# First value weights of attention split during the last projection unit, first attention scores held behind the value products

## The chip, the core and the metric

The kernel runs on one core of a Trainium2 chip. Its five engines each take instructions in order from a queue of their own: TensorE (PE, matrix products), VectorE (DVE), ScalarE (ACT), GpSimd (POOL) and SyncE (SP, which here only issues DMAs). They wait for one another through semaphores. The metric is device time in microseconds (us) of one execution, and lower is better.

## The reference, cut to what matters

The program is one decoder block on 1024 tokens of 1024 channels in float32. What bears on the change is how the projections feed attention:

```python
h = rmsnorm(x, norm_mix[i])
proj = h @ w_in[i]
qa, ka, va, qb, fb, ib, gb, gate_a, gate_b = jnp.split(proj, IN_SPLITS, axis=-1)
ya = dilated_attention(qa, ka, va)       # 8 heads of 64: softmax over masked scores q k^T, times v
yb = hgrn2(qb, fb, ib, gb, lb_all[i], hg_norm[i])
merged = jax.nn.sigmoid(gate_a) * (ya @ w_a_up[i]) + jax.nn.sigmoid(gate_b) * (yb @ w_b_up[i])
x = x + merged @ w_out[i]
# then a SwiGLU block, a per-layer embedding and a last norm
```

`va` has 512 columns. The kernel makes it in two halves of 256 columns.

## The kernel before, in words

**Split products.** Every float32 operand of a product is split into a high part in the fp32r format and a low part, the rest. A product is then three matmuls: high by high, high by low, low by high. For a weight block `weight` (lines 165 to 173) issues a DMA from HBM into a raw tile `wr`, POOL rounds it to the high part `wh` (L171), and DVE subtracts to get the low part `wl` (L172).

**Memory slots.** Big tiles lie in 49 slots of 4 KB per partition, s0 to s48. A `Ring` hands out a fixed list of slots in turn. A tile that gets a slot waits for everything that still reads or writes the slot's tile before it.

**Projection units.** Twenty column tiles of `w_in` go through ten Winograd units of two tiles each (`winograd`, `proj_unit`). A unit makes seven products of 12 matmuls each in the order 1, 5, 7, 2, 3, 4, 6 (`ORDER`), so product 7 is its third. The weight side of a product is a tile `q`, split on ACT (L299) and DVE (L300) into slots 3 to 7. The token side of products 5, 7, 4 and 6 lies in tiles `B`, split once at the start and read by all ten units. Those of product 7 are in slots 41 to 44, and the tenth unit is the last to read them. Products 3 and 7 write the two halves of one PSUM tile `u`. Between product 7 and the products that add to that tile, DVE reads it (L335, into `v`).

**After a unit** DVE and POOL add the products up (L771 to L781) into tiles `pj` in slots 40, 47 and 8, and SP stores them to HBM (L794). The last unit stores `hgq_dram`; its first `pj` lies in slot 8.

**Start of attention** (from L840). `qk_parts` loads queries and keys of a head back from HBM (`qr`, `kl`) and splits them on ACT (L471, L472) and DVE (L474, L475). `v_gemm(0, ...)` (L489) loads and splits two weight tiles of the first half of `va` (the high parts in the ring of slots 3, 4, 5, the low parts in that of 8, 6, 7) and makes eight tiles of 128 tokens. Each has 24 matmuls of 256 columns (L484 to L486), goes to one of three PSUM banks b0 to b2, and is moved out by ACT (L499) and DVE (L500). `attend_rows` makes scores of 128 queries (L525, L526) in the one PSUM tile `sp`; DVE adds the mask and takes the row minimum (L538), ACT takes exp (L542), DVE the reciprocal of the sum (L543), and POOL scales (L544). `attend_values` transposes such rows on PE (L565) and multiplies them with the values (L557, L558). `fill` puts matmuls of other products (here gates, L192 to L194) between these steps.

**What sets the order.** The Tile framework orders each engine's queue ahead of time, from dependencies and its own estimates of durations, not in the order in which the code is written. `tc.issue_after(ins)` asks that instructions of a block stand behind `ins` in the queue of the engine of `ins`.

Of the kernel before, what the change touches and what calls it, by code (L numbers as in the profile page):

```python
# [20 lines left out]
P = 128  # L21
# [23 lines left out]
SCALE_A, SCALE_B = 0.9, (1.6, 1.3, 1.3, 1.3, 1.0)  # L45
# [8 lines left out]
class Ring:  # L54
# [7 lines left out]
    def next(self, shape, dtype, name):  # L62
        tag = self.tags[self.n % len(self.tags)]
        self.n += 1
        Ring.count += 1
        return self.pool.tile(list(shape), dtype, tag=tag, name=f"{name}_{Ring.count}")
# [49 lines left out]
def drain(gen):  # L116
    for _ in gen:
        pass
# [11 lines left out]
def block_kernel(ctx: ExitStack, tc: tile.TileContext, a: dict, out: bass.AP):  # L130
    nc = tc.nc
    pe, dve, act, pool = nc.tensor, nc.vector, nc.scalar, nc.gpsimd
# [7 lines left out]
    def ring(ids):  # L140
        return Ring(sb, [f"s{i}" for i in ids])
# [9 lines left out]
    ones = cp.tile([P, P], F32, name="ones")  # L151
# [8 lines left out]
    def f32(t):  # L160
        return t.bitcast(F32)
# [4 lines left out]
    def weight(src, shape, hi_ring=None, lo_ring=None):  # L166
        raw = RAW.next(shape, F32, "wr")
        nc.sync.dma_start(raw, src)
        hi = (hi_ring or HI).next(shape, F32R, "wh")
        lo = (lo_ring or LO).next(shape, F32R, "wl")  # L170
        pool.tensor_scalar(hi, raw, 1.0, 0.0, ALU.mult, ALU.add)  # L171
        dve.tensor_sub(lo, raw, f32(hi))  # L172
        return hi, lo

    def weight_parts(src, shape):

        raw, hi, lo = RAW.next(shape, F32, "wr"), HI.next(shape, F32R, "wh"), LO.next(shape, F32R, "wl")

        def part(j):
            ks = slice(4 * j, 4 * j + 4)  # L180
            nc.sync.dma_start(raw[:, ks], src[:, ks])
            pool.tensor_scalar(hi[:, ks], raw[:, ks], 1.0, 0.0, ALU.mult, ALU.add)
            dve.tensor_sub(lo[:, ks], raw[:, ks], f32(hi)[:, ks])

        return (hi, lo), part
# [174 lines left out]

    warm = MS.next([P, 512], F32, "warm")
    for _ in range(WARM):
        pe.matmul(warm[:, :P], ones, ones, start=True, stop=True)
    w_start = [weight_parts(a["w_in"][20 + t], [P, KD, P]) for t in range(NTOGETHER)]
    both = ps.tile([P, 2, 512], F32, tag="sp", name="start")
    banks = [ps.tile([P, 512], F32, tag=t, name=f"start_{t}") for t in ("b0", "b1", "b2", "ov")]
# [6 lines left out]
    def start_rights(j, i):  # L373

        for k in {5: (i,), 7: (i + 4,)}.get(j, ()):
            act.activation(xr8[k], xr8[k], AF.Identity, scale=vec[:, V_MIX + k : V_MIX + k + 1])
        right[j][i] = RIGHT[j](xr8, i, 4, ring([TB[j][i]]))

    def latest(engine):

        return next(i for i in reversed(nc.cur_bb.bb.instructions) if i.engine == engine)
# [47 lines left out]
    with tc.issue_after(last_split), tc.issue_after(last_square.ins):  # L429
        for i in range(4):  # L430
            start_rights(5, i)
# [46 lines left out]
    def nat_gemm(b, wts, t):  # L478

        ts_ = slice(t * P, (t + 1) * P)  # L480
        for k in range(KD):
            hi, lo = wts[k // 4]
            xh, xl = xg[k]
            pe.matmul(b, xh[:, ts_], hi[:, k % 4, :], start=(k == 0), stop=False)  # L484
            pe.matmul(b, xh[:, ts_], lo[:, k % 4, :], start=False, stop=False)  # L485
            pe.matmul(b, xl[:, ts_], hi[:, k % 4, :], start=False, stop=(k == KD - 1))  # L486
            yield 3 * 0.107

    def v_gemm(half, vs):  # L489
        wts = [weight(a["w_v"][half, j], [P, 4, 256]) for j in range(2)]  # L490
        for t in range(NTOK):
            if t % 2 == 0:
                vs.append(VR.next([P, 2, 4, 2, 64], F32R, "v"))
            v = vs[-1]
            b = MM.next([P, 512], F32, "mm")[:, :256]
            yield from nat_gemm(b, wts, t)
            bv = b.rearrange("p (h d) -> p h d", h=4)
            r = rn[:, t : t + 1]
            act.activation(v[:, t % 2, :, 0, :], bv, AF.Identity, scale=r)  # L499
            dve.scalar_tensor_tensor(  # L500
                v[:, t % 2, :, 1, :], bv, r, f32(v)[:, t % 2, :, 0, :], op0=ALU.mult, op1=ALU.subtract
            )
# [12 lines left out]
    def attend_rows(g, qkh, rows):  # L515

        q, kh, kl = qkh
        pr2 = None
        for i in range(4 * g, 4 * g + 4):
            n = (i + 1) * P  # L520
            sp = ps.tile([P, S], F32, tag="sp", name=f"sp{Ring.count}")
            k0 = 0
            for w in SEG[i + 1]:
                ks = slice(k0, k0 + w)
                pe.matmul(sp[:, ks], q[:, i * P : i * P + P], kh[:, ks], start=True, stop=False)  # L525
                pe.matmul(sp[:, ks], q[:, i * P : i * P + P], kl[:, ks], start=False, stop=True)  # L526
                k0 += w
            if g:
                pr = PR[1].next([P, S], F32, "p")
            elif i % 2 == 0:  # L530
                pr2 = PR[0].next([P, 2, 512], F32, "p")
                pr = pr2[:, 0]
            else:
                pr = pr2[:, 1]
            m = sm.tile([P, 1], F32, tag="m", name="m")
            den = sm.tile([P, 1], F32, tag="den", name="den")
            rd = sm.tile([P, 1], F32, tag="rd", name="rd")
            dve.tensor_tensor_reduce(  # L538
                out=pr[:, :n], in0=sp[:, :n], in1=NB[:, S - n :], op0=ALU.add, op1=ALU.min,
                scale=1.0, scalar=3e38, accum_out=m,  # L540
            )
            act.activation(pr[:, :n], pr[:, :n], AF.Exp, bias=m, scale=-1.0, accum_out=den)  # L542
            dve.reciprocal(rd, den)  # L543
            pool.tensor_scalar(pr[:, :n], pr[:, :n], rd, 0.0, ALU.mult, ALU.add)  # L544
            rows.append(pr)
            yield Y_ROW[0] + Y_ROW[1] * (i + 1) / 8
# [202 lines left out]
    units = [(j, j + 1) for j in range(0, 20, 2)]  # L749
# [12 lines left out]
    def proj_dst(j):  # L762
        if j < 8:
            return qk_dram[j]
        return hg_dram["fg"[j % 2]][j // 2 - 4] if j < 16 else hg_dram["q"][j - 16]

    rn = cp.tile([P, NTOK], F32, name="rn")
    for tiles in units:
        done = dict(proj_unit(right, TG))
        e0, e1 = (EO.next([P, S], F32, "pj") for _ in range(2))  # L770
        dve.tensor_add(e0[:, c1], done[3], done[6])  # L771
        dve.tensor_add(e1[:, c0], done[4], done[6])
        pool.tensor_add(e1[:, c1], done[7], done[6])
        if tiles[0] < 8:

            dve.scalar_tensor_tensor(e0[:, c0], done[2], -0.125, rs[:, c0], op0=ALU.mult, op1=ALU.mult)
            dve.scalar_tensor_tensor(e0[:, c1], e0[:, c1], -0.125, rs[:, c1], op0=ALU.mult, op1=ALU.mult)
        else:
            dve.tensor_mul(e0[:, c0], done[2], rs[:, c0])
            dve.tensor_mul(e0[:, c1], e0[:, c1], rs[:, c1])  # L780
        pool.tensor_mul(e1, e1, rs)  # L781
        if 8 <= tiles[0] < 16:
            hd = tiles[0] // 2 - 4
            k = EO.next([P, S], F32, "k")
            act.activation(e0, e0, AF.Sigmoid)
            pool.tensor_scalar(e0, e0, oml[:, hd : hd + 1], lb[:, hd : hd + 1], ALU.mult, ALU.add)
            pool.tensor_scalar(k, e0, -1.0, 1.0, ALU.mult, ALU.add)
            nc.sync.dma_start(hg_dram["k"][hd], k)
            for cs in halves:
                sg = EV.next([P, 512], F32, "sg")  # L790
                act.activation(sg, e1[:, cs], AF.Sigmoid)
                dve.tensor_mul(e1[:, cs], e1[:, cs], sg)
        for j, e in zip(tiles, (e0, e1)):
            nc.sync.dma_start(proj_dst(j), e)  # L794
        if tiles[0] == 6:

            diag = EO.next([P, NTOK, P], F32, "diag")
            rs3 = rs.rearrange("p (n t) -> p n t", n=NTOK)
            dve.tensor_mul(diag, rs3, ident.unsqueeze(1).to_broadcast([P, NTOK, P]))
            dve.tensor_reduce(out=rn, in_=diag, axis=mybir.AxisListType.X, op=ALU.add)  # L800
# [31 lines left out]
    fill = Filler()  # L832
# [7 lines left out]
    qk, vs, vn = {}, ([], []), ([], [])  # L840
# [2 lines left out]
    MM = pring("b0", "b1", "b2")  # L843
    NB = ring([47]).next([P, S], F32, "nb")
    nc.sync.dma_start(NB, a["nb"])
    drain(v_gemm(0, vs[0]))
    RAW, HI, LO = ring([0, 1]), ring([3, 4]), ring([8, 6])
    rows = []
    add_gates(2)
    v_last = fill.add(v_gemm(1, vs[1]))  # L850
    fill.along(attend_rows(0, qk[0, 0], rows), SCALE_A)
    groups = [(p, h, g) for p in range(NPAIR) for h in range(2) for g in range(2)]
    for (p, h, g), after in zip(groups, groups[1:] + [None]):
        if (p, h, g) == (2, 0, 0):
# [17 lines left out]
        rows = next_rows  # L872
# [477 lines left out]
```

## Time and profile before

| what | us |
|---|---|
| three runs | 1670.85, 1673.15, 1665.83 |
| their median | 1670.85 |
| the profiled execution | 1667.34 |
| its span, from the first to the last instruction | 1665.5 |
| PE busy in the span | 1604.8 (96%) |
| DVE busy | 1117.4 (67%) |
| ACT busy | 649.5 (39%) |
| POOL busy | 559.9 (34%) |

The profiled execution lies 3.5 us under the median of the runs and within their spread. The page of the profile gives each engine's busy time; the timeline gives each instruction's start and length; the table by stage gives busy time and the clock that TensorE was granted (1.00 is 2.4 GHz, 0.50 is 1.2 GHz) in a stretch. A start is in us from the beginning of the span.

### The profile page before, as it was taken

The numbers are of one execution on the slowest core, as the hardware profiler recorded it, in microseconds if no ns is written. First come the engines' busy times: TensorE is split into PE (matmuls) and PEld (weight loads), VectorE is DVE, ScalarE is ACT, GpSimd is POOL, SyncE is SP. The second block draws the span as 40 slices with busy tenths as digits, with TensorE's granted clock in tenths as the row PEclk, the third lists the DMA queues.
The fourth block names the chain that finished last, engine by engine and source line by source line (L and its number), as shares of the span: only waits on it lengthen the run. The fifth ranks groups of instructions, "written<-read, shape, count | busy, mean of one in ns | idle before, by whom it ended". The sixth has DMA issues, their size and how long they took to land.

```text
span 1665.5 us, 21614 instructions
## 1 busy us (share of the span) xinstructions
PE 1604.8 (96%) x7968; PEld 1332.7 (80%) x7968; DVE 1117.4 (67%) x1673; ACT 649.5 (39%) x1128; POOL 559.9 (34%) x413
## 2 busy tenths in 40 slices
PE   9899998999999999999999999999999999998996
PEld 7687787898998888888887888888888778775786
DVE  8955664678665566765557666666777668798536
ACT  6523332467552011532345333333333554444334
POOL 2555652223322111114354343444554000034214
PEclk9999998999999999999999999999999999999998
DMA  5232343332124322533432323334444887654202
GB/s 197 76 115 102 139 157 116 96 90 72 52 92 146 109 102 77 196 133 114 153 113 83 113 90 99 111 114 140 152 140 163 276 292 232 233 154 128 63 1 101
DMA packets 84778, 213.54 MB, mean 128 GB/s; under 512 B 9408, under 2 KB 16320, under 8 KB 84672
## 3 DMA queue, kind: packets, MB, share of 16 engines
q1 hardware_dynamic: 84528, 212.14, 39.0%
q8 instruction: 62, 1.02, 0.3%
q14 instruction: 44, 0.36, 0.1%
q10 hardware_dynamic: 144, 0.02, 0.0%
HBM read 155.51 MB, written 56.62 MB: 127 GB/s over the span
## 4 chain that ended last, share of the span: by engine, by line
PE 47%; DVE 7%; DMA 4%; issue 2%; ACT 2%; POOL 1%; DVEq 0%; SPq 0%; POOLq 0%; ACTq 0%
PE u L275 8%; PE u L276 8%; PE u L277 8%; PE mm L194 5%; PE mm L192 5%; PE mm L193 5%; DVE B L236 2%; PE g L666 1%; DMA w<-w_dn 1%; DVE q L1028 1%; PE dnb L277 1%; PE dnb L275 1%; PE dnb L276 1%; DMA st<-t_dram 1%; DMA st<-first_dram 1%
## 5 line engine op out<-in xcount | busy, mean ns | idle before, releaser
L275 PE MATMUL u<-B,q 128*128 128x512 f32 x776 | 303.8, 394 | 5.6 <-ACT m L333 3.6
L276 PE MATMUL u<-B,q 128*128 128x512 f32 x776 | 304.4, 392 | 3.7 <-DVE B L236 3.7
L277 PE MATMUL u<-B,q 128*128 128x512 f32 x776 | 303.4, 391 | 1.9 <-DVE q L300 1.9
L275 PEld LDWEIGHTS u<-B,q 128*128 128x128 f32 x776 | 146.6, 189 | 41.5 <-ACT m L333 8.2
L276 PEld LDWEIGHTS u<-B,q 128*128 128x128 f32 x776 | 146.7, 189 | 35.4 <-DVE B L236 5.2
L277 PEld LDWEIGHTS u<-B,q 128*128 128x128 f32 x776 | 146.6, 189 | 32.9 <-DVE q L300 2.3
L299 ACT CAST q<-s 128x512 fp32r<-128x512 f32 x128 | 79.5, 622 | 157.6 <-PE u L277 145.6
L300 DVE TENSOR_TENSOR q<-s,q 128x512 fp32r<-128x512 f32 x128 | 107.5, 842 | 49.2 <-ACT q L299 48.1
L192 PE MATMUL mm<-xh,wh 128*128 128x512 f32 (+1 forms) x352 | 138.1, 392 | 0.1
L194 PE MATMUL mm<-xh,wl 128*128 128x512 f32 (+1 forms) x352 | 132.0, 375 | 1.8 <-DVE wl L172 1.7
L193 PE MATMUL mm<-xl,wh 128*128 128x512 f32 (+1 forms) x352 | 131.4, 373 | 0.0
L171 POOL TENSOR_SCALAR wh<-wr 128x1024 fp32r<-128x1024 f32 (+1 forms) x55 | 57.3, 1044 | 203.9 <-PE mm L193 100.1
L300 DVE TENSOR_TENSOR q<-w,q 128x512 fp32r<-128x512 f32 x96 | 85.0, 886 | 60.2 <-ACT q L299 60.0
L193 PE MATMUL mm<-l,wh 128*128 128x512 f32 (+1 forms) x296 | 115.0, 389 | 1.3 <-DVE l L910 0.9
L192 PE MATMUL mm<-h,wh 128*128 128x512 f32 (+1 forms) x296 | 114.7, 389 | 0.9 <-POOL wh L171 0.8
L194 PE MATMUL mm<-h,wl 128*128 128x512 f32 (+1 forms) x296 | 114.0, 386 | 1.0 <-DVE wl L172 1.0
L299 ACT CAST q<-w 128x512 fp32r<-128x512 f32 x96 | 59.7, 622 | 121.8 <-PE u L277 69.1
L544 POOL TENSOR_SCALAR p<-p,rd 128x128 f32<-128x128 f32 (+3 forms) x64 | 53.1, 831 | 144.3 <-DVE rd L543 126.4
L1082 POOL TENSOR_TENSOR us<-v 128x512 f32<-128x512 f32 x22 | 38.7, 1757 | 155.0 <-DVE v L337 142.2
L194 PEld LDWEIGHTS mm<-xh,wl 128*128 128x128 f32 x352 | 66.3, 188 | 14.5 <-DVE wl L172 3.1
L484 PE MATMUL mm<-wh,xh 128*128 128x256 f32 x256 | 76.4, 300 | 0.0
L485 PE MATMUL mm<-wl,xh 128*128 128x256 f32 x256 | 73.7, 288 | 0.8 <-DVE wl L172 0.8
(303 smaller groups left out, 3847.6 us busy)
## 6 DMA issues: line engine op xcount, KB each, us to landing
w<-w_gu SPq DMA_DIRECT2D x44, 512.0 KB, 3.9
w<-w_dn SPq DMA_DIRECT2D x72, 256.0 KB, 3.9
t_dram<-t SPq DMA_DIRECT2D x44, 256.0 KB, 4.3
w<-w_in SPq DMA_DIRECT2D x20, 512.0 KB, 3.8
st<-t_dram SPq DMA_DIRECT2D x20, 512.0 KB, 4.5
w<-w_dn SPq DMA_DIRECT2D x36, 192.0 KB, 3.8
wr<-w_in SPq DMA_DIRECT2D x13, 512.0 KB, 3.7
sg_dram<-gt SPq DMA_DIRECT2D x24, 256.0 KB, 2.0
```

The costliest lines, as they stand in the source:

```text
L171: pool.tensor_scalar(hi, raw, 1.0, 0.0, ALU.mult, ALU.add)
L192: pe.matmul(dst, hi[:, k, :], xh[:, c0 : c0 + n], start=first and k == ks[0], stop=False)
L193: pe.matmul(dst, hi[:, k, :], xl[:, c0 : c0 + n], start=False, stop=False)
L194: pe.matmul(dst, lo[:, k, :], xh[:, c0 : c0 + n], start=False, stop=last and k == ks[-1])
L275: pe.matmul(dst, q[:, 0, k], bh, start=first and not more and k == 0, stop=False, skip_group_check=more)
L276: pe.matmul(dst, q[:, 0, k], bl, start=False, stop=False, skip_group_check=more)
L277: pe.matmul(dst, q[:, 1, k], bh, start=False, stop=end, skip_group_check=more)
L299: act.copy(q[:, 0], left[m])
L300: dve.tensor_sub(q[:, 1], left[m], f32(q)[:, 0])
L484: pe.matmul(b, xh[:, ts_], hi[:, k % 4, :], start=(k == 0), stop=False)
L485: pe.matmul(b, xh[:, ts_], lo[:, k % 4, :], start=False, stop=False)
L544: pool.tensor_scalar(pr[:, :n], pr[:, :n], rd, 0.0, ALU.mult, ALU.add)
```

## The change

The two weight tiles of the first half of `va` are asked for before the last projection unit is written, and get slots of their own choice: the high parts 41 and 42, the low parts 43 and 44, which hold the token side of product 7 until the last unit has made it. `v_gemm` takes these tiles instead of loading its own. The name `values_made` is the last PE instruction of the eight value tiles, and the rows of the first group of scores stand behind it on PE.

```diff
     for _ in range(WARM):
-        pe.matmul(warm[:, :P], ones, ones, start=True, stop=True)
+        warm_up = pe.matmul(warm[:, :P], ones, ones, start=True, stop=True)
...
+    pe_engine = warm_up.ins.engine
...
-    def v_gemm(half, vs):
-        wts = [weight(a["w_v"][half, j], [P, 4, 256]) for j in range(2)]
+    def v_gemm(half, vs, wts=None):
+        wts = wts or [weight(a["w_v"][half, j], [P, 4, 256]) for j in range(2)]
...
     for tiles in units:
+        if tiles == units[-1]:
+
+            w_v0 = [weight(a["w_v"][0, j], [P, 4, 256], ring([41 + j]), ring([43 + j])) for j in range(2)]
         done = dict(proj_unit(right, TG))
...
-    drain(v_gemm(0, vs[0]))
+    drain(v_gemm(0, vs[0], w_v0))
+    values_made = latest(pe_engine)
     RAW, HI, LO = ring([0, 1]), ring([3, 4]), ring([8, 6])
     rows = []
     add_gates(2)
     v_last = fill.add(v_gemm(1, vs[1]))
-    fill.along(attend_rows(0, qk[0, 0], rows), SCALE_A)
+    with tc.issue_after(values_made):
+        fill.along(attend_rows(0, qk[0, 0], rows), SCALE_A)
```

No instruction is added to or taken from any engine. The queues differ only from the last unit to the first transposes of attention; behind that each engine's order is as before. Lines of the changed file stand two further down in `v_gemm` and `attend_rows` and five further down in the unit loop.

**PE where the last unit ends, before.** `mm` are value tiles (the first is `mm_288_1976`), `wl_283_1966` is the low part of the first weight tile, `sp` are scores of the first four rows, `pt0000` is the first transpose:

```order
L484 MATMUL mm_289_2003<-wh_282_1965,xh_13_111 128x256
L484 MATMUL mm_291_2031<-wh_282_1965,xh_13_111 128x256
L525 MATMUL sp298_2195<-kh_271_1924,q_270_1923 128x256 [waits DVE_49,Activation_49]
L526 MATMUL sp298_2195<-kl_272_1925,q_270_1923 128x256 [waits DMAHW6_49,DMAHW5_49,DVE_49]
L525 MATMUL sp304_2217<-kh_271_1924,q_270_1923 128x256 [waits DVE_49]
L526 MATMUL sp304_2217<-kl_272_1925,q_270_1923 128x256
L525 MATMUL sp304_2230<-kh_271_1924,q_270_1923 128x384 [waits DVE_49]
L526 MATMUL sp304_2230<-kl_272_1925,q_270_1923 128x384
L525 MATMUL sp305_2244<-kh_271_1924,q_270_1923 128x512 [waits DVE_49]
L526 MATMUL sp305_2244<-kl_272_1925,q_270_1923 128x512
L565 MATMUL pt0000_2277<-ident_69,p_299_2198 128x128 [waits DMAHW7_49,Pool_49]
L485 MATMUL mm_288_1976<-wl_283_1966,xh_13_111 128x256 [waits DVE_49]
```

**PE at the same place, now** (`u_267_1824` is product 6 of the last unit):

```order
L277 MATMUL u_267_1824<-B_74_528,q_273_1860 128x512
L486 MATMUL mm_288_1976<-wh_261_1813,xh_13_111 128x256 [waits Pool_49]
L487 MATMUL mm_288_1976<-wl_262_1814,xh_13_111 128x256
L488 MATMUL mm_288_1976<-wh_261_1813,xl_14_112 128x256
L486 MATMUL mm_288_1976<-wh_261_1813,xh_16_148 128x256
L487 MATMUL mm_288_1976<-wl_262_1814,xh_16_148 128x256
```

The value tiles now follow the unit without a score between them.

**PE where the value tiles end, now** (`mm_298_2168` is the eighth value tile, `mm_304_2213` a gate):

```order
L488 MATMUL mm_298_2168<-wh_264_1819,xl_42_324 128x256
L527 MATMUL sp298_2195<-kh_277_1936,q_276_1935 128x256 [waits Activation_49]
L528 MATMUL sp298_2195<-kl_278_1937,q_276_1935 128x256 [waits DMAHW7_49,DMAHW0_49]
L192 MATMUL mm_304_2213<-xh_13_111,wh_301_2208 128x512 [waits DVE_49,Pool_49]
L193 MATMUL mm_304_2213<-xl_14_112,wh_301_2208 128x512
L194 MATMUL mm_304_2213<-xh_13_111,wl_302_2209 128x512
L527 MATMUL sp304_2217<-kh_277_1936,q_276_1935 128x256 [waits DVE_49]
L528 MATMUL sp304_2217<-kl_278_1937,q_276_1935 128x256
L192 MATMUL mm_304_2213<-xh_16_148,wh_301_2208 128x512
L193 MATMUL mm_304_2213<-xl_17_149,wh_301_2208 128x512
L194 MATMUL mm_304_2213<-xh_16_148,wl_302_2209 128x512
L527 MATMUL sp304_2230<-kh_277_1936,q_276_1935 128x384 [waits DVE_49]
```

The first four rows of scores have moved here, with three or four gate matmuls behind each.

**DVE around the first value weights, before.** `wl_283_1966` stands between steps of the scores:

```order
L538 ISA p_305_2233,m_2234<-sp304_2230,nb_280_1961 128x384 [waits PE_49]
L538 ISA m_2234 128x1
L543 RECIPROCAL rd_2201<-den_2200 128x1 [waits Activation_49]
L475 TENSOR_TENSOR kl_277_1944<-kl_277_1944,kh_276_1943 128x512 [waits DMAHW7_49,DMAHW0_49,Activation_49]
L475 TENSOR_TENSOR kl_277_1944<-kl_277_1944,kh_276_1943 128x512 [waits Activation_49]
L172 TENSOR_TENSOR wl_283_1966<-wr_281_1963,wh_282_1965 128x1024 [waits DMAHW1_49,DVE_49]
```

**DVE around them, now** (`v_270_1827` is the read of the PSUM tile after product 7 of the last unit):

```order
L476 TENSOR_TENSOR q_281_1954<-qr_284_1959,q_281_1954 64x512 [waits DMAHW5_49,Activation_49]
L172 TENSOR_TENSOR wl_262_1814<-wr_260_1811,wh_261_1813 128x1024 [waits DMAHW6_49,PE_49,Pool_49]
L172 TENSOR_TENSOR wl_265_1820<-wr_263_1817,wh_264_1819 128x1024 [waits DMAHW6_49,PE_49,Pool_49]
L335 TENSOR_TENSOR v_270_1827<-u_268_1825,m_269_1826 128x512
L784 TENSOR_TENSOR pj_274_1925<-u_266_1823,rs_44_349 128x512 [waits DMAHW4_49,DMAHW0_49,PE_49]
```

Both low parts are now made inside the last unit, ahead of the read of product 7; the splits of the second head's keys have moved in among the steps that empty the value tiles.

## Rows read from the trace of the kernel before

**Rows 1.** The page: busy time, share of the span and instructions of TensorE.

```profile
PE 1604.8 (96%) x7968; PEld 1332.7 (80%) x7968; DVE 1117.4 (67%) x1673; ACT 649.5 (39%) x1128; POOL 559.9 (34%) x413
```

**Rows 2.** Table by stage, 260 to 280 us, with granted clock and DMA share.

```profile
core 0: us, PE busy (x) PEld busy (x) DVE busy (x) ACT busy (x) POOL busy (x), PEclk, DMA share, GB/s
...
260.00:265.00 5.00, 2.45 (x11) 1.72 (x9) 4.67 (x8) 1.97 (x5) 2.55 (x2) 0.91 0.89 212
265.00:270.00 5.00, 2.10 (x5) 1.29 (x5) 3.26 (x6) 3.13 (x7) 1.37 (x1) 0.50 0.80 279
270.00:275.00 5.00, 3.54 (x11) 2.25 (x11) 4.65 (x11) 2.04 (x5) 2.27 (x3) 0.50 0.28 86
275.00:280.00 5.00, 5.00 (x34) 5.00 (x33) 1.32 (x4) 0.98 (x2) 0.69 (x1) 0.73 0.41 136
```

**Rows 3.** Timeline of PE, last unit to value tiles: start, length, line, operation, [idle<-releaser].

```profile
248.56 0.43 PE L275 MATMUL u<-B,q 128*128 128x512 f32 x1
...
253.19 0.39 PE L275 MATMUL u<-xh,q 128*128 128x512 f32 x1
...
261.35 0.51 PE L484 MATMUL mm<-wh,xh 128*128 128x256 f32 x3
264.33 0.58 PE L525 MATMUL sp<-kh,q 128*128 128x256 f32 x1 [2.47 <-ACT kh L472]
266.98 0.58 PE L526 MATMUL sp<-kl,q 128*128 128x256 f32 x1 [2.06 <-DVE kl L475]
...
273.43 0.58 PE L485 MATMUL mm<-wl,xh 128*128 128x256 f32 x1 [0.59 <-DVE wl L172]
...
277.81 0.28 PE L484 MATMUL mm<-wh,xh 128*128 128x256 f32 x1
```

**Rows 4.** Timeline of PE where the value tiles end.

```profile
298.09 0.41 PE L192 MATMUL mm<-xh,wh 128*128 128x512 f32 x1
...
303.54 0.48 PE L192 MATMUL mm<-xh,wh 128*128 128x512 f32 x1
```

**Rows 5.** Timeline of DVE.

```profile
251.58 0.69 DVE L335 TENSOR_TENSOR v<-u,m 128x512 f32<-128x512 f32 x1 [0.52 <-PE u L277]
...
264.31 3.21 DVE L475 TENSOR_TENSOR kl<-kl,kh 128x512 fp32r<-128x512 f32 x2 [0.15 <-ACT kh L472]
...
272.07 1.31 DVE L172 TENSOR_TENSOR wl<-wr,wh 128x1024 fp32r<-128x1024 f32 x1
...
273.44 0.67 DVE L538 CUSTOM_DVE_ANT_0 p<-sp,nb 128x512 f32<-128x512 f32 x1
...
297.98 1.23 DVE L172 TENSOR_TENSOR wl<-wr,wh 128x1024 fp32r<-128x1024 f32 x1 [1.53 <-POOL wh L171]
```

**Rows 6.** Timeline of POOL.

```profile
251.70 1.05 POOL L171 TENSOR_SCALAR wh<-wr 128x1024 fp32r<-128x1024 f32 x1 [3.83 <-PE u L277]
...
263.71 2.66 POOL L781 TENSOR_TENSOR pj<-pj,rs 128x1024 f32<-128x1024 f32 x1
...
275.42 0.69 POOL L544 TENSOR_SCALAR p<-p,rd 128x512 f32<-128x512 f32 x1 [0.83 <-DVE rd L543]
...
298.34 1.78 POOL L171 TENSOR_SCALAR wh<-wr 128x1024 fp32r<-128x1024 f32 x1 [0.39 <-PE mm L486]
```

**Rows 7.** Timeline of ACT.

```profile
264.82 1.28 ACT L542 ACT_TABLE_LOAD   x1
...
274.14 0.72 ACT L542 ACTIVATE p<-p,m 128x512 f32<-128x512 f32 x1 [2.00 <-DVE m L538]
...
298.29 0.48 ACT L499 ACTIVATE v<-mm,rn 128x256 fp32r<-128x256 f32 x1 [2.36 <-PE mm L486]
```

**Rows 8.** Timeline of SP's DMA issues.

```profile
264.19 2.53 SPq L794 DMA_DIRECT2D hgq_dram<-pj  x2
...
267.28 6.46 SPq L168 DMA_DIRECT2D wr<-w_in  x2
```

**Rows 9.** Instructions on the tile kl, 240 to 300 us: its DMAs.

```profile
DMA to landing us min/median/max: 3.7/4.1/4.6
```

## The prediction

> **What bounds the kernel now.** I began with the busy times: PE works for 96% of the span [rows 1], so a change pays only where it takes away time in which PE waits or runs slowly. The table by stage shows one such place where the change acts. From 260 to 275 us PE is busy 2.45, 2.10 and 3.54 us of each 5, and its granted clock goes from 0.91 to 0.50, the lower of its two levels (1.2 GHz instead of 2.4); it is still 0.73 on average from 275 to 280, with PE busy all the time [rows 2]. The timeline of PE tells what lies in it. The last projection unit ends with a matmul just ahead of 261.35. Three value matmuls follow, the high by high ones, which need no low part. Then PE makes four rows of scores, waiting 2.47 us for a key split on ACT and 2.06 for one on DVE, and at 273.43 it goes on with the value tiles, when DVE has made the low part of the first weight tile [rows 3]. That split ran on DVE from 272.07 to 273.38 [rows 5]. Its slot, 8, is that of the last unit's first output, whose store is one of the two that SP issues from 264.19 on [rows 8]; in DVE's queue it stands behind steps of the scores. So PE is held by a memory slot and a place in a queue, not by a lack of work: the tokens that the value tiles need have been there for long.
>
> **What the stretch costs now.** I take it from 261.35 to the gate matmul at 303.54, behind the first transposes [rows 3, 4]. From there on each engine's queue is as before. It takes 42.19 us.
>
> **What the same work takes in the new order.** *Value tiles:* eight of 24 matmuls, 192. At full clock the pitch is read from 277.81 to 298.09: 189 of the 192 start at 273.43 or later, 20 of them ahead of 277.81, so 169 fill 20.28 us, 0.12 each [rows 3, 4]. 192 x 0.12 = 23.04 us. *What stands behind them:* from 298.09 to 303.54, 5.45 us with the fifth score row, 18 gate matmuls and three transposes [rows 4], stays. *The four score rows* join it: four matmuls of 256 columns at 0.12, two of 384 at 0.18 and two of 512 at 0.24 (in proportion to the pitch above), 1.32 us, and about 0.08 for the transpose that stood in the hole. Sum 23.04 + 5.45 + 1.40 = 29.9 us, so 42.19 - 29.9 = 12.3 us come free if nothing new waits. Of these some 2.0 us are clock alone: 20 matmuls from 273.43 to 277.81 took 4.38 us, where 20 x 0.12 are 2.4 [rows 3].
>
> **New wait one: the unit's third product.** The splits now come on DVE ahead of L335, which reads product 7 out of its PSUM tile, and product 3, which adds to that tile, waits for that. Before, L335 ran at 251.58 for 0.69 us [rows 5] and product 3 began at 253.19 [rows 3]. In the new queue four matmuls of product 6 stand ahead of product 3 (4 x 0.23 = 0.9), so it is wanted at 254.1. Best case: the first high part starts when product 7's first three matmuls have read slot 41, about 249.5 (they start at 248.56 [rows 3]), POOL needs 1.05 for each [rows 6], DVE 1.23 for each low part [rows 5], from about 251.1, behind the key split in front of them; L335 then ends near 254.2, and product 3 waits 0.1 us. Worst case: POOL starts at 251.70 as before, its two splits end at 253.8, no low part overlaps the second of them, and L335 ends at 253.8 + 1.23 + 1.23 + 0.69 = 256.95, a wait of 2.9 us. PE has freed slot 41 more than a microsecond before 251.70, so I stand near the best case: 0.8 us. Whether splits of the two engines overlap matters here, and rows show that they don't: a high part on POOL beside a low part on DVE took 1.78 us instead of 1.05 (298.34, beside 297.98), and two key splits on DVE took 3.21 us beside a POOL multiply of 2.66 [rows 5, 6]. The Trainium skill (SBUF — State Buffer, section "SBUF: two separate sides") has the rule for this: a DVE instruction with two SBUF inputs and a GpSimd one that reads SBUF take turns on a shared port for the whole instruction. By that rule the wait would be 0.7 us, since the first low part would start only when the second high part is done; with free overlap it would be 0.1. The rows agree with the rule, and it speaks a little against this change.
>
> **New wait two: softmax of the first rows.** The four rows no longer run in the hole. If T is the start of the first score, the last value tile leaves ACT from T + 0.2 for 0.48 us (298.29 against 298.09 [rows 4, 7]). Then the exp table is loaded, 1.28 us, which before ran at 264.82 while PE was idle anyway [rows 7]: T + 2.0. The fourth row is scored behind three rows and ten gate matmuls, about T + 3.2; two matmuls of it and DVE's 0.67 us [rows 5] make T + 4.5. Exp takes 0.72 [rows 7] and some 0.1 to read the sum, the reciprocal about 0.2, POOL 0.69 [rows 6]: T + 6.4. PE meanwhile has 5.45 + 1.32 us less the transposes' 0.3, and reaches the fourth row's transpose at T + 6.5 less a little. So the cover is just long enough, and I put 0.4 us here, between 0 and 1.8 (the whole table load and one exp late). The Trainium skill (ScalarE: Activation LUTs, section "What ACT_TABLE_LOAD costs") gives a load of 1283 ns, with which the row of 1.28 agrees, but a drain of about 1380 ns on top. By that the chain would be ready at T + 7.8, and the gain would be about 1.4 us smaller; before, ACT waited for DVE after the load, so no row here shows a drain.
>
> **Moved at no cost.** The DMAs of the weights keep their places on SP. Two more splits on POOL, of the next gate weights, stand ahead of the last unit's multiplies; their loads go out when the low parts are made, about 254, and take some 4 us, so POOL (1.05 us for each) is free again near 260, before the unit ends. Cover gone, each us there would delay only the last stores. The clock stays at 1.00 through the value tiles if PE has no hole.
>
> **Sum.** 12.3 - 0.8 - 0.4 = 11.1 us. Against the profiled execution that is 1667.34 - 11.1 = 1656.2; against the median of the runs, which lies 3.5 higher, 1659.8. The mean of all four times is 1669.3, and I take 1669.3 - 11.1 = **1658.2 us**.
>
> **The rivals.**
> *The first softmax is laid bare.* In the trace the first rows took from 264.33 [rows 3] to the end of POOL's 0.69 at 275.42 [rows 6], 11.8 us. If they take as long again, PE's cover of 6.5 leaves 5.3 us of waiting, and the clock falls once more, 2.0 us. Gain 12.3 - 0.8 - 5.3 - 2.0 = 4.2, time 1665.1, no change by the bound below. For it: each row waits for the one PSUM tile. Against it: over 4 us of the 11.8 were waits for keys [rows 3], which will be there by then. 14%.
> *The weights still come late*, because a split sits behind something in DVE's or POOL's queue, so that the first value tile waits some 6 us: 1664.2. For it: worst case above. Against it: all in front of the splits ran by 251.1. 6%.
> *Slower: value tiles starve.* Key splits of the second head now stand on ACT and DVE between the reads of value tiles 3 and 4, their loads partly behind the last two stores on SP. There are three banks, so tile 7 needs tile 4 out by 261.35 + 0.8 + 6 x 2.88 = 279.4; each us later costs one. The stores were issued from 264.19 for 2.53 us [rows 8] and such loads landed at most 4.6 us after issue [rows 9], so about 272. At 290.5 the gain is gone, from 299 on the kernel is over 0.5% slower; at 300 it takes 1669.3 - 11.1 + 20.6 = 1678.8. 4%.
>
> **How the numbers follow.** My forecast has 76%. 0.5% of the time, 8.4 us, is about what a measurement of this kernel can tell from no change. The forecast's gain lies between 12.3 - 0.1 = 12.2 and 12.3 - 2.9 - 1.8 = 7.6, and the runs of before spread over 7 us, so about a tenth of it falls within 0.5%: faster 0.72 (with a little from the rivals' better ends), same 0.24, slower 0.04. Low end: the lowest run less the best gain, 1665.83 - 12.2, about 1653.5. High end: the bare softmax, 1665.
>
> **What would show it.** Right: PE goes from the unit to the low-part matmuls without a gap near 262; clock 1.00 from 260 to 285; value tiles leave every 2.88 us and end near 285; the first transposes stand near 291.5 with under 1 us of waiting; span about 11 us shorter. Product 3's start less 254.1 gives the first wait. Wrong: a gap in front of the first transposes with a lower clock (bare softmax), or of value matmuls at 279 (starved banks), or the same saving at 303 that is lost again further down.

## The result, and the profile after

| kernel | median us | lowest to highest | runs | ratio to before, 95% interval |
|---|---|---|---|---|
| before | 1671.25 | 1665.83 to 1677.06 | 11 | |
| changed | 1659.31 | 1653.24 to 1665.77 | 11 | 0.9933 [0.9917, 0.9950] |

The change makes the kernel faster: the whole interval of the ratio lies below 1. The ratio is worth 1671.25 x 0.0067 = 11.2 us, between 8.4 and 13.9; 11.1 us were forecast, and the median lies 1.1 us above the forecast of 1658.2.

The profiled execution of the changed kernel took 1665.77 us, the longest of its eleven, and its span is 1664.0 us, only 1.5 us under that of before. A comparison of the two spans would therefore mislead, and I compare stretch by stretch. Each start below is that of a matmul: the first of product 7 of the last unit (in before at 248.56 [rows 3]), the gate behind the first transposes (303.54 [rows 4]), the first `g` of the gated recurrence, and the first and last L275 matmul of the down stage (`dnb`). The changed kernel was profiled a second time (`e3_again`, below), and a run without the hold (`e1_split_only`) has the same queues on every engine.

| stretch, us | before | changed | changed, again | without the hold |
|---|---|---|---|---|
| start to product 7 | 248.56 | 251.52 | 249.38 | 249.27 |
| product 7 to the gate | **54.98** | **43.53** | **43.54** | **43.56** |
| gate to first `g` | 226.4 | 225.5 | 225.7 | 226.0 |
| first `g` to down stage | 769.7 | 771.8 | 770.8 | 771.6 |
| down stage, first to last matmul | 219.4 | 223.8 | 220.0 | 224.1 |
| from there to the end | 146.5 | 147.8 | 146.4 | 148.0 |

All of the gain lies in the one stretch that the change touches, 11.45 us, and it is there to 0.03 us in three executions. The other stretches differ as much between executions with equal queues (220.0, 223.8 and 224.1 in the down stage) as they do between before and changed, so no payback shows in them. That is no proof of none: two of the three executions with the new queues are 7 to 8 us longer behind the gate than before, one is 0.9 us longer. The whole runs decide it better. The ratios of the three sets of runs with these queues (this one, `e3_again` and `e1_split_only`) are worth 11.2, 10.7 and 10.2 us against 11.4 to 11.5 won in the stretch, so 7 us aren't paid back; a loss of a microsecond or two would lie within their intervals.

The first `g`, with which all kernels below can be compared, is the first of these groups (count, shortest, median and longest in ns, first and last start), in before and in the changed kernel:

```profile
L652 PE MATMUL g<-q,k x64: 270/275/275, 529.9 to 662.6; 128*128 128x128 f32 x64
L654 PE MATMUL g<-q,k x64: 270/275/275, 520.6 to 653.2; 128*128 128x128 f32 x64
```

It stands 281.4 us behind product 7 before and 269.1 now.

PE in the changed kernel, timeline (start, length, line, operation, idle time and its releaser), from product 7 to the gate:

```profile
251.52 0.43 PE L275 MATMUL u<-B,q 128*128 128x512 f32 x1
...
257.89 0.50 PE L275 MATMUL u<-xh,q 128*128 128x512 f32 x1 [0.67 <-DVE v L335]
...
265.27 0.28 PE L486 MATMUL mm<-wh,xh 128*128 128x256 f32 x1
265.39 0.28 PE L487 MATMUL mm<-wl,xh 128*128 128x256 f32 x1
...
288.31 0.28 PE L527 MATMUL sp<-kh,q 128*128 128x256 f32 x1
...
294.70 0.60 PE L567 MATMUL pt<-ident,p 128*128 128x128 f32 x4
295.05 0.48 PE L192 MATMUL mm<-xh,wh 128*128 128x512 f32 x1
```

Where before had three value matmuls, a hole and the scores [rows 3], the second value matmul is now the low-part one at 265.39, and no value matmul waits. The eight value tiles take 288.31 - 265.27 = 23.04 us, which is 192 matmuls at full clock. The one new wait is the 0.67 us ahead of product 3. By the starts it is more, since a matmul's recorded length (0.39 us) is longer than the step to the next one (0.23): from product 7 to the first value matmul the unit takes 265.27 - 251.52 = 13.75 us, against 261.35 - 248.56 = 12.79 before, 0.96 longer. The table by stage of the same kernel shows it from the side of the clock; its rows answer [rows 2]:

```profile
core 0: us, PE busy (x) PEld busy (x) DVE busy (x) ACT busy (x) POOL busy (x), PEclk, DMA share, GB/s
260.00:265.00 5.00, 5.00 (x23) 4.14 (x23) 2.69 (x3) 1.14 (x2) 2.12 (x2) 1.00 0.11 38
265.00:270.00 5.00, 5.00 (x42) 4.92 (x42) 3.93 (x7) 1.58 (x3) 3.67 (x2) 1.00 0.96 265
270.00:275.00 5.00, 5.00 (x44) 5.00 (x44) 3.51 (x5) 0.98 (x3) 0.36 (x1) 1.00 0.73 208
275.00:280.00 5.00, 5.00 (x44) 5.00 (x43) 2.56 (x5) 2.12 (x5) 0.00 (x0) 1.00 0.70 220
```

PE is busy all 20 us at a clock of 1.00 (2.4 GHz), where before it was busy 13.1 of 20 and fell to 0.50 [rows 2]. The weight splits of the changed kernel, and the read of product 7 behind them (POOL first, then DVE), answer [rows 5, 6]:

```profile
252.51 2.52 POOL L171 TENSOR_SCALAR wh<-wr 128x1024 fp32r<-128x1024 f32 x2 [1.69 <-PE u L277]
```

```profile
254.14 3.09 DVE L172 TENSOR_TENSOR wl<-wr,wh 128x1024 fp32r<-128x1024 f32 x2
257.16 0.68 DVE L335 TENSOR_TENSOR v<-u,m 128x512 f32<-128x512 f32 x1
```

Both low parts are ready at 257.2, 8 us ahead of the first value matmul.

### The profile page after: what moved, and what is told of

The parts are those of the page before. It is cut to its first block, busy times and chain, and to the rows that moved or that the text cites. A ratio compares the mean times of both kernels' runs of the same rounds, so it can differ in the third digit from the quotient of the medians.

```text
span 1664.0 us, 21613 instructions
## 1 busy us (share of the span) xinstructions
PE 1606.4 (97%) x7968; PEld 1335.9 (80%) x7968; DVE 1119.0 (67%) x1673; ACT 649.0 (39%) x1128; POOL 559.0 (34%) x413
## 4 chain that ended last, share of the span: by engine, by line
PE 46%; DVE 8%; DMA 5%; issue 2%; ACT 1%; POOL 1%; DVEq 0%; SPq 0%; POOLq 0%; ACTq 0%
PE u L275 8%; PE u L277 8%; PE u L276 8%; PE mm L194 5%; PE mm L192 5%; PE mm L193 5%; DVE B L236 2%; DMA st<-t_dram 2%; DVE q L1035 1%; DMA w<-w_dn 1%; PE g L668 1%; DMA st<-first_dram 1%; POOL sb L933 1%; DMA st<-second_dram 1%; PE dnb L275 1%
## 5 line engine op out<-in xcount | busy, mean ns | idle before, releaser
L275 PE MATMUL u<-B,q 128*128 128x512 f32 x776 | 304.1, 395 | 7.0 <-ACT m L333 5.1
L275 PEld LDWEIGHTS u<-B,q 128*128 128x128 f32 x776 | 147.1, 190 | 42.0 <-ACT m L333 9.1
L299 ACT CAST q<-s 128x512 fp32r<-128x512 f32 x128 | 79.5, 622 | 157.7 <-PE u L277 146.4
L192 PEld LDWEIGHTS mm<-xh,wh 128*128 128x128 f32 x352 | 67.4, 192 | 9.3 <-issue 0.7
```

Source lines behind the costliest of these rows:

```text
L192: pe.matmul(dst, hi[:, k, :], xh[:, c0 : c0 + n], start=first and k == ks[0], stop=False)
L275: pe.matmul(dst, q[:, 0, k], bh, start=first and not more and k == 0, stop=False, skip_group_check=more)
L299: act.copy(q[:, 0], left[m])
```

## The experiments

**The hold taken away.** The weights keep their new slots and their early request; the scores are no longer held behind the value products. `e1_split_only`, against the changed kernel:

```diff
-    with tc.issue_after(values_made):
-        fill.along(attend_rows(0, qk[0, 0], rows), SCALE_A)
+    fill.along(attend_rows(0, qk[0, 0], rows), SCALE_A)
```

> The changed kernel without the hold: the first scores are free to go anywhere on TensorE. Its queues on all five engines come out row for row as those of the changed kernel. Theory (the slots of the first value weights carry the whole gain, the hold does nothing once they are early): value tiles follow the last unit without a gap, ratio to the kernel before 0.993, within noise of the changed kernel. Rival (the hold carries part of it): over 4 us slower than the changed kernel.

Measured: 1657.48 us, ratio 0.9939 [0.9920, 0.9959], and 43.56 us from product 7 to the gate. The hold does nothing here: with the early weights in their new slots, the framework puts the scores behind the value tiles by itself.

**The hold alone.** The weights keep their old slots and are asked for after the unit. `e2_hold_only`, against before (`pe_engine` is defined as in the changed kernel):

```diff
     drain(v_gemm(0, vs[0]))
+    values_made = latest(pe_engine)
...
-    fill.along(attend_rows(0, qk[0, 0], rows), SCALE_A)
+    with tc.issue_after(values_made):
+        fill.along(attend_rows(0, qk[0, 0], rows), SCALE_A)
```

> The kernel before with the hold alone: the first value weights keep their old slots, the scores stand behind the value tiles. The queues show the low part of the first weight tile on VectorE behind the splits of two heads' keys and ahead of all score steps. Theory (memory slot 8 and its store are what TensorE waits for): TensorE stops near 262 after three value matmuls and goes on near 270 instead of 273.4, first at the lower clock as before, so the stretch to the first transposes is some 2 us shorter than before: ratio 0.998 to 1.000. Rival (scores standing in front are the cause): value tiles go on by 264 and the gain is 9 us or more, ratio 0.994.

Measured: 1666.26 us, ratio 0.9986 [0.9971, 1.0000]. PE of this kernel, timeline:

```profile
260.81 0.51 PE L486 MATMUL mm<-wh,xh 128*128 128x256 f32 x3
269.38 0.58 PE L487 MATMUL mm<-wl,xh 128*128 128x256 f32 x1 [8.05 <-DVE wl L172]
...
294.15 0.28 PE L527 MATMUL sp<-kh,q 128*128 128x256 f32 x1
```

DVE of the same kernel:

```profile
263.54 4.65 DVE L477 TENSOR_TENSOR kl<-kl,kh 128x512 fp32r<-128x512 f32 x4
268.11 1.21 DVE L172 TENSOR_TENSOR wl<-wr,wh 128x1024 fp32r<-128x1024 f32 x1
```

PE has nothing else to do in the hole and waits 8.05 us. It goes on 21.36 us behind product 7's start (248.02 here), against 273.43 - 248.56 = 24.87 before, 3.5 us earlier, because the steps of the scores no longer stand ahead of the low part on DVE. The score rows, moved behind the value tiles, take 1.0 us of that back, the clock 0.1. What is left is what the trace shows: the first transposes stand 52.36 us behind product 7's start, against 54.7 before. In the changed kernel that is 43.18. The 9.2 us between them are the hole (8.2 by the starts) and 2.1 of lower clock in the value matmuls (189 of them in 24.77 us, where 189 x 0.12 = 22.68), less the 0.96 us that the changed kernel's unit takes longer and 0.2 in the score rows. In this kernel these transposes come ahead of the fifth score row, in the other two behind it; up to the first `g` it is 279.0 us, against 281.4 before and 269.1 in the changed kernel. So the rival is out: without the slots, holding the scores back wins 2.4 us of 12.3.

**The changed kernel once more.** `e3_again` is the changed kernel without an edit.

> The changed kernel once more, unaltered, for a second trace. Theory (the gain is all in the stretch up to the first transposes, and what the first trace lost behind it is scatter of single executions): the stretch from the end of the last unit to the transposes is again 30 to 31 us against 42.2, and the stretches behind it take other lengths than in the first trace. Rival (part of the gain is paid back in the feed-forward and down stages): these stages are again about 6.5 us longer than in the trace of the kernel before. Ratio 0.993 in both.

Measured: 1657.66 us, ratio 0.9936 [0.9921, 0.9951], with a span of 1655.8, 9.7 us under before's. From the end of the unit to the gate it takes 292.92 - 263.13 = 29.8 us, as in the first execution and a little under the 30 to 31 that were expected. The matmuls of the down stage, grouped as above, in the changed kernel:

```profile
L275 PE MATMUL dnb<-B,q x165: 387/389/792, 1292.4 to 1516.2; 128*128 128x512 f32 x165
```

and in the second execution of it:

```profile
L275 PE MATMUL dnb<-B,q x165: 388/390/505, 1289.4 to 1509.4; 128*128 128x512 f32 x165
```

Same queues, 223.8 against 220.0 us. What PE waited for there in the first of the two (total us, times, longest),

```profile
PE dnb L275 <- ACT q L1034: 3.3, 1, 3.3
```

and its table by stage (columns as above):

```profile
1440.00:1450.00 10.00, 6.66 (x25) 5.09 (x25) 8.53 (x15) 3.83 (x7) 0.00 (x0) 0.88 0.69 215
```

The same two views of the second:

```profile
PE dnb L275 <- ACT q L1034: 1.6, 1, 1.6
```

```profile
1440.00:1450.00 10.00, 8.42 (x36) 6.13 (x35) 7.73 (x13) 5.21 (x9) 0.00 (x0) 1.00 0.66 213
```

At the same place one execution waited 3.3 us and lost clock, the other 1.6 and did not. With the 2.1 us by which product 7 started later (251.52 against 249.38) that is 5.9 of the 8.2 us between the two spans. The new slots aren't needed for such a wait: `e10_hold_busy`, below, which has the weights in their old slots, waits 3.0 us at this place and loses clock too:

```profile
1440.00:1450.00 10.00, 6.95 (x24) 4.84 (x24) 8.12 (x14) 4.41 (x8) 0.00 (x0) 0.89 0.76 252
```

Why such a wait differs from one execution to the next isn't settled by these runs.

**The slots alone.** No hold and no early request: the weights are asked for after the unit, as before, but get slots 41 to 44. `e5_other_slots`, against before (`v_gemm` takes `wts` as in the changed kernel):

```diff
-    drain(v_gemm(0, vs[0]))
+    w_v0 = [weight(a["w_v"][0, j], [P, 4, 256], ring([41 + j]), ring([43 + j])) for j in range(2)]
+    drain(v_gemm(0, vs[0], w_v0))
```

> The kernel before, with only the slots of the first value weights altered: 41 and 42 for the high parts, 43 and 44 for the low ones; they are asked for behind the last unit, where they were, and there is no hold. The queues show the value tiles right behind the unit, the scores behind the value tiles, and the read of product 7 ahead of both low parts on VectorE. Theory (the slots alone do it): no wait of product 3, so the stretch is about 1 us shorter than in the changed kernel, 12.4 us shorter than before; ratio to before 0.9925, at most 1 us better than the changed kernel. Rival (the early request matters): a gap of several us between unit and value tiles, ratio 0.996 or more.

Measured: 1658.10 us, ratio 0.9944 [0.9924, 0.9964], 43.30 us from product 7 to the gate. The slots alone bring the gain. The expectation was wrong about the queue: one low part still stands ahead of the read of product 7. DVE of this kernel:

```profile
252.17 1.95 DVE L172 TENSOR_TENSOR wl<-wr,wh 128x1024 fp32r<-128x1024 f32 x1
254.04 0.68 DVE L335 TENSOR_TENSOR v<-u,m 128x512 f32<-128x512 f32 x1
254.64 1.21 DVE L172 TENSOR_TENSOR wl<-wr,wh 128x1024 fp32r<-128x1024 f32 x1
```

and PE, at product 3:

```profile
254.78 0.50 PE L275 MATMUL u<-xh,q 128*128 128x512 f32 x1 [0.42 <-DVE v L335]
```

So a part of the wait at product 3 is left, and it is smaller with fewer splits ahead of the read: 0.67 us idle with two, 0.42 with one. From product 7 to the first value matmul it is 263.07 - 249.56 = 13.51 us, against 13.75 with two and 12.79 before.

**Both low parts behind the read.** The slots are altered as in the run before, and the two weights' splits may stand on DVE only behind the read of product 7. `e7_split_behind_read`, against `e5_other_slots`:

```diff
+    reads = []
...
-                    dve.tensor_add(m57, b3, kept[5])
+                    reads.append(dve.tensor_add(m57, b3, kept[5]))
...
-    w_v0 = [weight(a["w_v"][0, j], [P, 4, 256], ring([41 + j]), ring([43 + j])) for j in range(2)]
+    with tc.issue_after(reads[-1].ins):
+        w_v0 = [weight(a["w_v"][0, j], [P, 4, 256], ring([41 + j]), ring([43 + j])) for j in range(2)]
```

> As the kernel with only the slots altered, but both low parts held on VectorE behind the read of the last unit's product 7; the queue shows read, low part, low part. Theory (what the early low parts cost the unit is their place ahead of that read, one for one): from the first matmul of product 7 to the first value matmul 12.8 us as in the kernel before, against 13.75 in the changed kernel and 13.5 with only the slots altered; no other wait. Total about 1 us under the changed kernel, which is too little to be told in whole runs (ratio 0.9925 to 0.994). Rival (product 3 waits for something else, such as the port that POOL holds): still 13.4 us or more.

Measured: 1656.56 us, ratio 0.9920 [0.9903, 0.9938]. DVE of this kernel:

```profile
251.26 0.69 DVE L337 TENSOR_TENSOR v<-u,m 128x512 f32<-128x512 f32 x1 [0.43 <-PE u L277]
251.87 2.35 DVE L172 TENSOR_TENSOR wl<-wr,wh 128x1024 fp32r<-128x1024 f32 x2
```

and POOL:

```profile
249.23 2.51 POOL L171 TENSOR_SCALAR wh<-wr 128x1024 fp32r<-128x1024 f32 x2 [1.69 <-PE u L277]
```

The read now runs first, product 3 doesn't wait, and the first value matmul stands 12.79 us behind product 7's start, to the hundredth what it was before (261.35 - 248.56), against 13.75 in the changed kernel. The gate follows at 42.56 us, 0.97 earlier than in the changed kernel. In whole runs that can't be separated: the intervals overlap.

**Only the low parts moved.** `e8_low_slots` leaves the high parts in slots 3 to 5 and gives the two low parts slots 43 and 44, against before:

```diff
-        wts = [weight(a["w_v"][half, j], [P, 4, 256]) for j in range(2)]
+        wts = [weight(a["w_v"][half, j], [P, 4, 256], None, ring([43 + j]) if half == 0 else None) for j in range(2)]
```

> The kernel before with only the two low parts of the first value weights in slots 43 and 44; the high parts stay in the ring of slots 3 to 5, the request stays behind the unit, no hold. Theory (slot 8 of the low part is the whole cause of the hole): no gap between unit and value tiles, and the low parts come behind the read of product 7, so 12.8 us from product 7 to the first value matmul and about 42.6 us from there to the gate matmul behind the first transposes (before 55.0, changed 43.5); ratio 0.993. Rival (the high parts' slots matter too): a gap of a microsecond or more in front of the value tiles.

Measured: 1656.25 us, ratio 0.9920 [0.9900, 0.9940]. This one line, with no hold and no early request, gives all of the gain. DVE of this kernel:

```profile
252.95 0.69 DVE L335 TENSOR_TENSOR v<-u,m 128x512 f32<-128x512 f32 x1 [0.52 <-PE u L277]
254.15 1.23 DVE L172 TENSOR_TENSOR wl<-wr,wh 128x1024 fp32r<-128x1024 f32 x1 [0.52 <-POOL wh L171]
...
256.33 1.22 DVE L172 TENSOR_TENSOR wl<-wr,wh 128x1024 fp32r<-128x1024 f32 x1 [0.35 <-POOL wh L171]
```

PE of this kernel, where the value tiles begin:

```profile
262.72 0.28 PE L484 MATMUL mm<-wh,xh 128*128 128x256 f32 x1
```

The low parts now wait for POOL alone, and both are made behind the read and inside the unit; the first value matmul stands 262.72 - 249.93 = 12.79 us behind product 7's start, and PE waits nowhere from there to the transposes. The high parts never had to move. The order of scores, gates and first transposes is another here, so that the gate behind them isn't the same mark: it stands 43.17 us behind product 7's start, where 42.6 were expected. Up to the first `g` it is 268.9 us, against 269.1 in the changed kernel and 281.4 before.

**Only the first low part moved.** `e9_first_low_slot` gives slot 43 to the first low part; the second then gets slot 8.

```diff
-        wts = [weight(a["w_v"][half, j], [P, 4, 256]) for j in range(2)]
+        wts = [weight(a["w_v"][half, j], [P, 4, 256], None, ring([43]) if (half, j) == (0, 0) else None) for j in range(2)]
```

> The kernel before with only the first low part in slot 43. The second low part is then the next to take slot 8. Theory (whoever holds slot 8 waits for the last unit's store): the three first value tiles run their first half, 36 matmuls more than before, then the scores, and TensorE waits for the second low part until about 272; 33 matmuls are done earlier and part of the lower clock is spared, so some 5 to 7.5 us of the 12 are won, ratio 0.9955 to 0.997. Rival (only the first low part matters): no wait at the second, ratio 0.993.

Measured: 1661.96 us, ratio 0.9951 [0.9937, 0.9965]. PE of this kernel:

```profile
265.22 0.28 PE L525 MATMUL sp<-kh,q 128*128 128x256 f32 x1
...
270.50 0.58 PE L485 MATMUL mm<-wl,xh 128*128 128x256 f32 x1 [0.40 <-DVE wl L172]
```

DVE of this kernel, the second low part:

```profile
269.22 1.22 DVE L172 TENSOR_TENSOR wl<-wr,wh 128x1024 fp32r<-128x1024 f32 x1
```

and its table by stage (columns as above):

```profile
265.00:270.00 5.00, 2.65 (x12) 1.38 (x10) 3.69 (x9) 2.80 (x10) 0.64 (x1) 1.00 0.49 171
270.00:275.00 5.00, 4.60 (x26) 4.50 (x26) 3.89 (x11) 1.82 (x6) 2.05 (x4) 0.66 0.43 129
```

The hole moves on with slot 8: 39 value matmuls run without it, then PE turns to the scores again and resumes at 270.50. These 5.28 us hold 1.3 us of scores at full pitch, and the clock is 0.66 in the 5 us behind 270. The first `g` stands 273.4 us behind product 7's start, between before (281.4) and changed (269.1). That is 8.0 us won, and the ratio gives 8.2; both lie a little over what was expected (5 to 7.5 us, 0.9955 to 0.997). The rival is out: the second low part has its own wait.

**The hole kept, PE busy in it.** `e10_hold_busy` is the hold alone with 34 idle matmuls (the trace records each twice) between the first value matmul and the next, into a bank that is free; their result is read by nobody.

```diff
+    keep = [34]
...
             pe.matmul(b, xh[:, ts_], hi[:, k % 4, :], start=(k == 0), stop=False)
+            if keep and k == 0 and t == 0:
+                idle = ps.tile([P, 512], F32, tag="ov", name="idle")
+                for _ in range(keep.pop()):
+                    pe.matmul(idle[:, :P], ones, ones, start=True, stop=True)
```

> The kernel with the hold alone, plus 34 matmuls of ones by ones in the hole in front of the value tiles (about 7 us of work that nothing reads, in a PSUM bank that is free there). Theory (some 2 us of what the hole costs are clock): the hole ends where it did, about 21.4 us behind the first matmul of product 7, but the granted clock stays at or near 1.00 and the 189 value matmuls behind it take 22.7 us instead of 24.7: about 2 us shorter than with the hold alone, ratio to before 0.9965 to 0.998. Rival (the clock is set by something else): still 24.7 us at 0.5 to 0.6.

Measured: 1664.36 us, ratio 0.9970 [0.9955, 0.9984]. PE of this kernel:

```profile
260.67 7.76 PE L492 MATMUL idle<-ones 128*128 128x128 f32 x68
...
269.12 0.39 PE L493 MATMUL mm<-wl,xh 128*128 128x256 f32 x1 [0.47 <-DVE wl L172]
...
291.90 0.28 PE L533 MATMUL sp<-kh,q 128*128 128x256 f32 x1
```

The table by stage (columns as above), first with the idle matmuls,

```profile
270.00:275.00 5.00, 5.00 (x44) 5.00 (x44) 1.17 (x2) 1.02 (x3) 0.00 (x0) 1.00 0.59 200
```

and of the hold alone:

```profile
270.00:275.00 5.00, 5.00 (x29) 5.00 (x29) 0.69 (x1) 0.52 (x3) 0.00 (x0) 0.60 0.57 179
```

PE goes on at the same time in both, 21.4 us after the start of product 7. But behind that 44 value matmuls start in 5 us instead of 29, and the 189 of them take 291.90 - 269.12 = 22.78 us, against 24.77. So 2.0 us of the hole's price is clock, and the rest is the wait itself. Up to the first `g` it is 277.0 us, against 279.0. This rests on the two traces: in whole runs the intervals of the two ratios overlap.

## Why the prediction was right, point by point

**What was to be won: right.** The value tiles took 23.04 us, as summed. The stretch got 11.45 us shorter, where the sum gave 11.1. The difference, term by term: the unit takes 0.96 us longer instead of 0.8 (-0.16), the first transposes don't wait at all instead of 0.4 (+0.4), and the score rows with their fillers take 288.31 to 295.05, 6.74 us, instead of 5.45 + 1.40 = 6.85 (+0.11). The 2.0 us named as clock alone are what the idle matmuls gave back.

**The wait at product 3: right in cause and in size.** The prediction named its own measure, product 3's start less 254.1. Carried over by the 2.96 us by which product 7 started later, it is 257.89 - 2.96 - 254.1 = 0.83 us, where 0.8 was put. The unit lost 0.96, 0.1 more, because the first matmul behind the wait took 0.34 us to the next one instead of 0.23. The first high part started 1.0 us after product 7's first matmul (252.51 - 251.52), as in the best case, so slot 41 was free as early as assumed. The first low part started 2.6 us behind product 7 (254.14 - 251.52), near the best case of 2.5. What made it 0.83 and not 0.1 is the length of DVE's pair: 3.09 us instead of 2 x 1.23 = 2.46 [rows 5]. POOL's second high part ran until 255.03, for 0.89 us beside it; in `e7_split_behind_read`, where POOL is done 0.13 us before the pair starts, it takes 2.35. POOL's pair took 2.52 us, where one takes 1.05 [rows 6], but not because of the low parts, since in `e7_split_behind_read` it takes 2.51 all the same. There as here a query split of 0.77 to 0.78 us ran on DVE beside it; that this is the reason isn't shown by a run of its own. DVE and POOL instructions that lengthen each other like this are what the Trainium skill (SBUF — State Buffer, section "SBUF: two separate sides") describes: two such instructions take turns on a shared port. The trace agrees in size: 0.83 measured, 0.7 by that rule, 0.1 without it. The runs with one and with no split ahead of the read show that the queue's order is the cause.

**The first softmax: right.** With T = 288.31, POOL finished the fourth row at 294.06 + 0.70 = T + 6.45 (estimated T + 6.4), and the transposes began at T + 6.39 without a wait. The terms of that estimate, as they are listed, add up to only T + 6.2 (4.5 + 0.72 + 0.1 + 0.2 + 0.69). The cover was just long enough. ACT of the changed kernel, timeline:

```profile
288.51 0.47 ACT L501 ACTIVATE v<-mm,rn 128x256 fp32r<-128x256 f32 x1 [2.36 <-PE mm L488]
289.00 1.28 ACT L544 ACT_TABLE_LOAD   x1
290.30 0.40 ACT L544 ACTIVATE p<-p,m 128x128 f32<-128x128 f32 x1
```

The load starts 0.02 us behind the instruction in front of it, and exp starts 0.02 us behind the load. The drain of about 1380 ns that the Trainium skill names (ScalarE: Activation LUTs, section "What ACT_TABLE_LOAD costs") doesn't show here on either side, so the gain wasn't made smaller by it; the measurement decides. The prediction had no row for it, since ACT waited for DVE behind the load [rows 7]. The trace of before has one further up: the load at 164.42 starts 0.02 us behind the instruction in front of it, takes 1.28 us, and the sigmoid behind it starts at 165.71.

**The rivals.** The softmax wasn't bare, in three executions with these queues. It was argued down too far, though: of the waits for keys, "over 4 us of the 11.8", the 2.47 us lie ahead of 264.33, where the 11.8 us begin [rows 3], so only 2.06 are part of them. The weights didn't come late. The value tiles didn't starve: DVE emptied value tile 4 at 278.33 in the changed trace, where the latest harmless time, carried over into that trace, is 279.4 + 2.96 + 0.16 = 282.5, and the tiles left ACT every 2.7 to 3.1 us.

**What it had not seen.** It priced the early request, the hold and the four slots as one change and didn't ask which of them does the work. What it read of slot 8 and its store [rows 8] held the answer: with the two low parts moved out of the ring of 8, 6, 7 everything else follows. And "a memory slot and a place in a queue" were two causes in a row rather than one. The slot decided where the framework put the split; at run time, in before and in the kernel with the hold alone, it started right behind an instruction on DVE that had kept DVE busy, and not on the store's landing. SP issues of the run with the hold alone:

```profile
263.66 2.53 SPq L796 DMA_DIRECT2D hgq_dram<-pj  x2
```

The first of the two stores is that of slot 8. These stores landed 2.6 to 3.0 us after their issue, so this one between 266.3 and 266.7, and the split started at 268.11. The store thus set a bound 1.4 to 1.9 us ahead of the start that was seen. In before the store went out at 264.19 and the split started at 272.07. No run keeps slot 8 and puts the split ahead of the key splits, so what the store alone would cost isn't measured.

**The later stages.** The prediction named a saving that is lost again further down as a sign of being wrong, but gave it no chance and no price. No such loss shows in the second execution (all stretches behind the gate together 1362.9 us, before 1362.0). In the first they are 7.0 us longer, 4.4 of them in the down stage, and without the hold 7.7. Since `e3_again` has the same queues, the change doesn't bring these 7 us with it; a loss of a microsecond or two isn't ruled out.

## What to carry to other kernels

When an engine waits for a small preparing step whose inputs have been there for long, look up which earlier tile its output slot held and what still reads that tile; another slot, freed earlier, can be the whole remedy, and holds or early requests around it may add nothing. Where the step is moved early, put it behind the reads on its engine that free a PSUM tile for TensorE: two splits ahead of one read cost 0.96 us here, and behind it none. One profiled execution may be the longest of its kernel: compare the touched stretch between fixed marks, and profile the same kernel twice before a loss elsewhere is put down to a change.

## What the runs showed of the hardware

- A hole of 8.05 us on TensorE cost another 2.0 us by the clock in the matmuls behind it, and matmuls that compute nothing of use took those 2.0 us away (`e2_hold_only`, `e10_hold_busy`). A run of shorter waits did so too: with PE busy 2.65 of 5 us, the clock was 0.66 in the next 5 (`e9_first_low_slot`).
- In the down stage PE waited at one place for 0.8 us in before, for 1.6, 2.5 and 3.3 in three executions with queues equal to the changed kernel's, and for 3.0 in `e10_hold_busy`. With 1.6 the clock stayed at 1.00 in the 10 us from 1440; with 2.5, 3.0 and 3.3 it was 0.83, 0.89 and 0.88. The length of the stage doesn't follow this one wait: with 3.0 it was 220.6 us, with 3.3 it was 223.8.
- DVE splits and POOL instructions beside them lengthened each other. Two key splits on DVE took 1.29 us in before with POOL idle (260.17); four took 4.65 in the run with the hold alone, where an addition of 2.66 us ran on POOL beside the first of them. One low part took 1.95 us with 0.88 us of POOL's high part beside it (`e5_other_slots`), and 1.21 without. In before, a high part on POOL took 1.78 us beside a low part on DVE, and 1.05 without [rows 5, 6].
